# The opening's conditioning products: split tiles, another order of transfers

## The chip, the cores and the metric

The kernel runs on one NeuronCore of a Trainium2 chip. Its engines are TensorE (PE, matrix products), VectorE (DVE), ScalarE (ACT), GpSimd (POOL) and SyncE (SP, which issues most transfers). The metric is the device time of one execution in microseconds (us), lower is better, as a median of several runs.

## The reference

One step of a decoder layer over 2048 prompt positions and 8 sample rows, model width 1024. All is float32:

```
shift1,scale1,g1,shift2,scale2,g2 = silu(c) @ w_ada + b_ada      # c: 1 + 8 rows, w_ada: 1024 x 6144
h  = RMSNorm(x)*(1+scale1)+shift1
[u | q | k | v | a_pool | a_attn] = h @ w_in
x += g1 * ( sig(a_pool)*(PoolMix(u) @ w_pool_br) + sig(a_attn)*(DilatedAttn(q,k,v) @ w_attn_br) ) @ w_out
h2 = RMSNorm(x)*(1+scale2)+shift2
x += g2 * relu(h2 @ w_up)^2 @ w_down
```

The first line is the conditioning. Its 6144 columns make twelve blocks of 512. Blocks 0 and 1 are shift1, blocks 2 and 3 are scale1: block 0 and block 2 serve the channels of h's rows 0 to 3 (a row is 128 channels), blocks 1 and 3 those of rows 4 to 7. Only these four are needed before h exists; the other eight follow much later.

## The kernel before

Large products are done as three single-rate (float32r) products of split operands, high by high, high by low and low by high (`mm3`, lines 157 to 168); a weight tile is split by an ACT cast and a subtraction (`load_w`, lines 178 to 185). PE's order is written out by hand: it is the order of the `PE` calls in the code. The other engines' queues are ordered by the compiler from the code and its own planning, and each queue runs in order. SP issues the transfers. Weights come through `weights`, which loads one tile ahead from a fixed plan.

The work is done channel-major in two halves of the positions (`ci`); each half has two column groups, in the first half of 512 and 520 columns (`HALVES`; the 520 include the 8 samples). `opening` (line 723) runs ahead of the first half's q, k, v products. It does, for block b of 0, 2, 1, 3:

- `ada_load`: four transfers of 512 KB (a chunk: 128 x 1024, two row groups of the contraction) into raw tiles, of which there are eight;
- `ada_rows`: eight full float32 products of 9 rows (silu of c) by 512 columns, straight from the raw tiles, into one PSUM bank, and a copy to `arow`, a single buffer;
- `mod_block`, later in PE's order: four small products that turn the 9 x 512 row into columns; DVE adds the bias, and for blocks 2 and 3 forms the scales `scg`.

Between them stand the sum of squares of x (`x_sum`: ACT squares, DVE additions), its finish (`rms_finish`: a product with ones, square root, reciprocal), `make_h` (x times rs on DVE, scale and shift on ACT, a cast on ACT, a subtraction on DVE for even and POOL for odd rows), and `part(t)`: the first four of eight contraction steps of the four first q and k tiles, twelve products each, for 512 columns. The function returns the four open PSUM tiles; `qkv` then adds the other four steps (48 products), evicts each tile by two ACT instructions (L381, L382), and goes on with the 520 columns.

PE's order in the opening: block 0, sum of rs0, transposes of 0, block 2, its transposes, block 1, part 0, transposes of 1, part 1, block 3, sum of rs1, part 2, transposes of 3, part 3. The order of loads in the code: block 0, first columns of x, block 2, block 1, w_in, second columns of x, block 3.

A float32 product counts as two MATMUL records in the trace, so a block has 16 `ps_ada` records here.

Of the kernel before, what the change touches and what calls it, by code (L numbers as in the profile page):

```python
# [8 lines left out]
F32 = mybir.dt.float32  # L9
F32R = mybir.dt.float32r  # L10
AF = mybir.ActivationFunctionType
ALU = mybir.AluOpType
# [4 lines left out]
P = 128  # L17
D = 1024
KD = 8
# [10 lines left out]
HS_AT = 6500  # L30
ADA_GAP = 3600
DEPTH_O = 1
R1 = 2

BRS = (
# [79 lines left out]
def emit(tc, I, O):  # L115
    nc = tc.nc
    V, S, G, PE, SP = nc.vector, nc.scalar, nc.gpsimd, nc.tensor, nc.sync
# [3 lines left out]
    def pool(stack, name, bufs=1, space=None, side=None):  # L121
        kw = {}
        if space is not None:
            kw["space"] = space
        elif side is not None:
            kw["side"] = side
        if space is not DRAM:
            kw["reuse_waits"] = "tile"
        return stack.enter_context(tc.tile_pool(name=name, bufs=bufs, **kw))
# [5 lines left out]
    stp = pool(top, "stp", 2, PSUM)  # L135
# [13 lines left out]
    def first():  # L149
        return tc.high_priority(offset=PRIO)  # L150

    def mm(ps, w, x, start, stop, ns):
        PE.matmul(ps, w, x, start=start, stop=stop)  # L153
        od.spent(ns)
# [13 lines left out]
    def small(ps, w, x, ns=220.0):  # L168
        mm(ps, w, x, True, True, ns)
# [8 lines left out]
    def load_w(src, eng=G, rp=None, hq=None, n=1024, tag="wh"):  # L178
        raw = (rp or rawp).tile([P, 1024], F32, tag="wr", name="wr")
        SP.dma_start(out=raw[:, :n], in_=src)  # L180
        wt = (hq or hlp).tile([P, 2, n], F32R, tag=tag, bufs=1 if n < 1024 else None, name="wh")
        with first():
            S.copy(out=wt[:, 0, :n], in_=raw[:, :n])  # L183
            eng.tensor_tensor(out=wt[:, 1, :n], in0=raw[:, :n], in1=wt[:, 0, :n].bitcast(F32), op=ALU.subtract)  # L184
        return wt
# [27 lines left out]
    def weights(*key):  # L213

        i = issued[0] - len(ready)
        assert plan[i] == key, (plan[i], key)
        while issued[0] < len(plan) and issued[0] <= i + depth[0]:
            k = plan[issued[0]]
            src = I[k[0]][k[1]] if len(k) == 2 else I[k[0]][k[1], :, k[2] * 1024:(k[2] + 1) * 1024]
            ready.append(load_w(src, G, *(extra if issued[0] == 3 else ())))  # L220
            issued[0] += 1
        return ready.pop(0)
# [4 lines left out]
    cv = {}  # L227
    off = 0
    for name, shape in CPACK:
        n = int(np.prod(shape))  # L230
# [7 lines left out]
    cT, ident, ones, hones, mask = cv["cT"], cv["ident"], cv["ones"], cv["hones"], cv["mask"]  # L238
# [5 lines left out]
    sil = cst.tile([P, KD, 9], F32, name="sil")  # L244
    silr = cst.tile([P, KD, 2, 9], F32R, name="silr")
# [10 lines left out]
    def mod_block(b, row, nr, idn, psp, tag):  # L256

        pt = psp.tile([P, 512], F32, tag=tag, name="ps_mt")
        for j in range(4):
            small(pt[:, j * 9:(j + 1) * 9], row[0:nr, j * P:(j + 1) * P], idn)  # L260
        V.tensor_tensor(out=mod[:, 4 * b:4 * b + 4, :], in0=pt[:, 0:36].rearrange("p (j r) -> p j r", j=4),
                        in1=bada[:, 4 * b:4 * b + 4].to_broadcast([P, 4, 9]), op=ALU.add)
        for i, lo in ((0, 8), (1, 32)):
            j = 4 * b - lo
            if j in (0, 4):
                V.scalar_tensor_tensor(out=sc[:, i, j:j + 4, :], in0=mod[:, 4 * b:4 * b + 4, :], scalar=1.0,
                                       in1=gn[:, i, j:j + 4].to_broadcast([P, 4, 9]), op0=ALU.add, op1=ALU.mult)
# [23 lines left out]
    def rms_sum(np_, acc, x, n, first, eng):  # L291
        sq = np_.tile([P, 520], F32, tag="sq", bufs=3, name="sq")
        if first:
            S.activation(out=acc[:, :n], in_=x, func=AF.Square)
        else:
            S.activation(out=sq[:, :n], in_=x, func=AF.Square)
            eng.tensor_tensor(out=acc[:, :n], in0=acc[:, :n], in1=sq[:, :n], op=ALU.add)

    def rms_finish(np_, psp, acc, splits):
        rs = np_.tile([P, 520], F32, tag="rs", bufs=1, name="rs")  # L300
        for c0, n in splits:
            ps = psp.tile([P, 512], F32, tag="st", name="ps_st")
            small(ps[:, :n], ones, acc[:, c0:c0 + n], n / 0.6)
            S.activation(out=rs[:, c0:c0 + n], in_=ps[:, :n], func=AF.Sqrt, scale=1.0 / D, bias=epsc)
            V.reciprocal(out=rs[:, c0:c0 + n], in_=rs[:, c0:c0 + n])
        return rs
# [16 lines left out]
    mmp = pool(ps1, "mmp", 6, PSUM)  # L323
# [5 lines left out]
    def hx(hb, nk, c0, n):  # L329
        return [(hb[:, k, 0, c0:c0 + n], hb[:, k, 1, c0:c0 + n]) for k in range(nk)]  # L330
# [9 lines left out]
    def x_sum(ci, hi, xs, eng):  # L340
        n = HALVES[ci][hi][1]
        acc = npl.tile([P, 520], F32, tag="ssum", bufs=1, name="ssum")
        for k in range(KD):
            rms_sum(npl, acc, xs[k], n, k == 0, eng)
        return acc

    def make_h(ci, hi, xs, rs, hb, ks=range(KD)):
        c0, n, splits = HALVES[ci][hi]
        for k in ks:
            hf = npl.tile([P, 520], F32, tag="sq", bufs=3, name="hf")  # L350
            modulated(hf, xs[k], xs[k], rs, n, 0, k, hb, c0, ci == 0 and hi == 1, G if k % 2 else V)
# [8 lines left out]
    def new_h():  # L360
        return hp.tile([P, KD, 2, 1032], F32R, tag="h", name="h")
# [332 lines left out]
    h0 = new_h()  # L694

    def load_x0(op, hi):
        c0, n, _ = HALVES[0][hi]
        xt = op.tile([P, KD, 520], F32, tag="x0", bufs=2, name="x0")
        for k in range(0, KD, 2):
            SP.dma_start(out=xt[:, k:k + 2, :n], in_=I["xT"][k:k + 2, :, c0:c0 + n].rearrange("k p n -> p k n"))  # L700
        return [xt[:, k, :n] for k in range(KD)]

    def ada_load(op, b):
        out = []
        for kk in range(4):
            raw = op.tile([P, 1024], F32, tag="wr", bufs=8, name="wr")
            SP.dma_start(out=raw, in_=I["w_ada"][b, kk])
            out += [raw[:, 0:512], raw[:, 512:1024]]
        return out

    def ada_rows(op, b, raws):
        ps = mmp.tile([P, 512], F32, tag="mm", name="ps_ada")
        for k in range(KD):
            mm(ps[0:9, :], sil[:, k, :], raws[k], k == 0, k == KD - 1, 860.0)
        row = op.tile([9, 512], F32, tag="arow", bufs=1, name="arow")
        with first():
            S.copy(out=row, in_=ps[0:9, :])
        return lambda: mod_block(b, row, 9, ident[0:9, 0:9], stp, "st")

    def opening():  # L720

        ost = ExitStack()
        op = pool(ost, "open", side="left")
        raws = {0: ada_load(op, 0)}
        x0 = load_x0(op, 0)
        raws[2] = ada_load(op, 2)
        raws[1] = ada_load(op, 1)
        keys = [("w_in", 8 + 6 * qk + i) for qk in range(2) for i in range(2)]
        ws, pss = [weights(*keys[0])], []
        x1 = load_x0(op, 1)  # L730
        raws[3] = ada_load(op, 3)
        hxs = hx(h0, KD, 0, 512)

        def part(t):
            if t:
                ws.append(weights(*keys[t]))
            pss.append(mmp.tile([P, 512], F32, tag="mm", name="ps_qk"))
            mm3(pss[t], wk(ws[t], KD)[:4], hxs[:4], False, stop=False)

        m0 = ada_rows(op, 0, raws[0])  # L740
        acc = x_sum(0, 0, x0, V)
        rs0 = rms_finish(npl, stp, acc, HALVES[0][0][2])
        m0()
        m2 = ada_rows(op, 2, raws[2])
        m2()
        make_h(0, 0, x0, rs0, h0, range(4))
        m1 = ada_rows(op, 1, raws[1])
        acc = x_sum(0, 1, x1, V)
        part(0)
        m1()  # L750
        part(1)
        m3 = ada_rows(op, 3, raws[3])
        rs1 = rms_finish(op, stp, acc, HALVES[0][1][2])
        part(2)
        m3()
        make_h(0, 0, x0, rs0, h0, range(4, KD))
        make_h(0, 1, x1, rs1, h0)
        part(3)
        ost.close()
        return ws, pss  # L760

# [15 lines left out]
    for _ in range(2):  # L777
        b, kk = todo.pop(0)
# [51 lines left out]
    mmp = pool(psa, "mma", 2, PSUM)  # L830
# [371 lines left out]
    mmp = pool(ps3, "mm3", 6, PSUM)  # L1202
# [46 lines left out]
    def up(ci, f, hi, wt, hb):  # L1249
        c0, n, splits = HALVES[ci][hi]  # L1250
        rt = fp.tile([P, 2, 520], F32R, tag="rt", bufs=6, name="rt")
        for a, l in splits:
            ps = mmp.tile([P, 512], F32, tag="mm", name="ps_up")
            dense(ps, wt, hb, a, l)
            r1 = fp.tile([P, 512], F32, tag="r1", bufs=R1, name="r1")
            with first():
# [32 lines left out]
    for ci in range(2):  # L1289
# [15 lines left out]
        br = od.spawn(branches(ci, 1, hbs[1], GAP_B), 3000)  # L1305
        depth[0] = DEPTH_O
        acc = project(ci, 0, hbs[0], xa, load_xa)
# [11 lines left out]
        for fb in range(1, 16):  # L1319
            if fb == 1:  # L1320
                rts = [r0[2:], [r1[2], up(ci, 3, 1, weights("w_up", 3), hbs[1])]]
            else:
                rts = [[], []]
                for f in (2 * fb, 2 * fb + 1):
                    wt = weights("w_up", f)
# [123 lines left out]
```

## Time and profile before

| | us |
|---|---|
| median of 3 runs | 3072.97 (3070.19 to 3075.37) |
| profiled execution | 3068.15 |
| its span | 3066.3 |
| PE busy in the span | 2956.4 (96%) |
| DVE, ACT, POOL busy | 1590.4, 970.6, 960.6 |
| mean granted TensorE clock | 0.982 |

The span goes from the first to the last instruction. In the page's 40 slices of 77 us PE is at 7 tenths in the first, which holds the opening, and at 9 in most others; transfers move 239 GB/s in the first slice.

### The profile page before, as it was taken

The page shows a single profiled execution, that of the slowest core. Times are in us where ns is not written, and L with a number is a line of the kernel's source. Part 1 is how long each engine was busy: PE and PEld are TensorE (multiplying, and loading weights), DVE is VectorE, ACT ScalarE, POOL GpSimd, SP SyncE. Part 2 cuts the span into 40 slices and gives each one's busy share as a digit, 9 for nine tenths or more (in the row PEclk, how much of TensorE's full clock was granted, in tenths as well). Part 3 has the DMA queues.
Part 4 walks back from the last instruction along what each step waited for, and adds up shares of the span by engine and source line. Part 5 has one row for each costly group of instructions (what it writes and reads, how often), then busy time and mean ns, then how long its engine had stood idle before and what let it go on. Part 6 is the DMA issues. An engine that isn't in the chain of part 4 may idle for free.

```text
span 3066.3 us, 40880 instructions
## 1 busy us (share of the span) xinstructions
PE 2956.4 (96%) x16220; PEld 2526.4 (82%) x16220; DVE 1590.4 (52%) x2645; ACT 970.6 (32%) x1765; POOL 960.6 (31%) x504
## 2 busy tenths in 40 slices
PE   7999999999898799999999999999999999999999
PEld 3899788887787688887899999999877788888887
DVE  5656442542744524447865555545578554444444
ACT  4333332434544434433521221221235212111211
POOL 2565341433433311224531222122245312221221
PEclk9999999999899889999999999999999999999999
DMA  6544752335777878876221111111272211111111
GB/s 239 176 139 156 275 174 91 129 107 151 198 191 209 186 191 217 235 233 236 94 96 35 56 49 46 45 49 49 84 250 83 76 42 56 48 49 42 55 43 68
DMA packets 204431, 379.09 MB, mean 124 GB/s; under 512 B 43232, under 2 KB 99904, under 8 KB 203456
## 3 DMA queue, kind: packets, MB, share of 16 engines
q1 hardware_dynamic: 192720, 359.63, 38.2%
q10 hardware_dynamic: 11520, 16.85, 1.5%
q8 instruction: 128, 2.10, 0.3%
q14 instruction: 63, 0.52, 0.1%
HBM read 294.89 MB, written 81.75 MB: 123 GB/s over the span
## 4 chain that ended last, share of the span: by engine, by line
PE 77%; DMA 6%; DVE 5%; issue 3%; ACT 2%; POOL 2%; SPq 1%; DVEq 0%; ACTq 0%; POOLq 0%
PE ps_dn L153 22%; PE ps_up L153 22%; PE ps_g L153 9%; PE ps_qk L153 5%; PE ps_v L153 4%; PE ps_wo L153 4%; PE ps_u L153 3%; PE ps_s L153 2%; PE ps_o L153 1%; PE ps_pb L153 1%; POOL wh L184 1%; PE ps_ada L153 1%; PE ps_ab L153 1%; DMA t1d<-ta 1%; DMA cs<-in_rope 1%
## 5 line engine op out<-in xcount | busy, mean ns | idle before, releaser
L184 POOL TENSOR_TENSOR wh<-wr,wh 128x1024 fp32r<-128x1024 f32 (+1 forms) x274 | 650.1, 2380 | 1679.0 <-ACT wh L183 1607.5
L153 PE MATMUL ps_dn<-rt,wh 128*128 128x512 f32 (+2 forms) x3840 | 726.2, 350 | 6.4 <-POOL wh L184 3.3
L153 PEld LDWEIGHTS ps_dn<-rt,wh 128*128 128x128 f32 x3840 | 618.9, 188 | 109.2 <-POOL wh L184 4.2
L183 ACT CAST wh<-wr 128x1024 fp32r<-128x1024 f32 (+1 forms) x306 | 309.4, 1023 | 730.7 <-issue 562.3
L1274 DVE SCALAR_TENSOR_TENSOR xa<-ps_dn,mod,xa 128x512 f32<-128x512 f32 (+1 forms) x640 | 405.2, 641 | 202.8 <-PE ps_dn L153 201.0
L153 PE MATMUL ps_g<-h,wh 128*128 128x512 f32 (+2 forms) x1920 | 390.5, 355 | 0.4 <-POOL wh L184 0.4
L153 PE MATMUL ps_up<-hb,wh 128*128 128x264 f32 (+2 forms) x2304 | 371.5, 320 | 0.0
L153 PE MATMUL ps_up<-ha,wh 128*128 128x512 f32 x1536 | 365.7, 394 | 0.0
L153 PEld LDWEIGHTS ps_up<-hb,wh 128*128 128x128 f32 x2304 | 332.3, 188 | 36.0
L153 PEld LDWEIGHTS ps_g<-h,wh 128*128 128x128 f32 x1920 | 309.4, 191 | 48.4 <-POOL wh L184 0.9
L153 PEld LDWEIGHTS ps_up<-ha,wh 128*128 128x128 f32 x1536 | 287.1, 188 | 64.2 <-issue 0.5
L153 PE MATMUL ps_qk<-h,wh 128*128 128x512 f32 (+2 forms) x1440 | 301.1, 363 | 8.9 <-POOL h L318 6.5
L1258 DVE TENSOR_TENSOR r<-r 128x512 f32<-128x512 f32 (+2 forms) x160 | 99.3, 620 | 387.0 <-ACT r L1257 386.9
L153 PEld LDWEIGHTS ps_qk<-h,wh 128*128 128x128 f32 x1440 | 235.9, 194 | 50.8 <-POOL h L318 7.5
L1260 DVE TENSOR_TENSOR rt<-r,rt 128x512 fp32r<-128x512 f32 (+2 forms) x160 | 217.8, 1361 | 81.8 <-ACT rt L1259 81.7
L1257 ACT ACTIVATE r<-ps_up 128x512 f32<-128x512 f32 (+2 forms) x160 | 82.1, 513 | 415.0 <-PE ps_up L153 415.0
L153 PE MATMUL ps_v<-wh,h 128*128 128x256 f32 (+1 forms) x1224 | 169.3, 294 | 24.5 <-ACT wh L183 18.9
L153 PEld LDWEIGHTS ps_v<-wh,h 128*128 128x128 f32 (+1 forms) x1224 | 155.2, 192 | 30.2 <-ACT wh L183 19.3
L914 ACT ACTIVATE pe<-pe,ost 128x128 f32<-128x128 f32 (+1 forms) x192 | 87.1, 455 | 153.2 <-DVE ost L912 149.9
L912 DVE CUSTOM_DVE_ANT_0 pe<-ps_s,cp 128x128 f32<-128x128 f32 (+1 forms) x192 | 61.4, 358 | 129.7 <-PE ps_s L153 129.7
L1259 ACT CAST rt<-r 128x512 fp32r<-128x512 f32 (+2 forms) x160 | 85.8, 536 | 66.3 <-DVE r L1258 66.3
L153 PE MATMUL ps_pb<-py,wh 128*128 128x512 f32 (+2 forms) x480 | 95.5, 358 | 6.6 <-ACT py L555 3.7
(181 smaller groups left out, 2985.4 us busy)
## 6 DMA issues: line engine op xcount, KB each, us to landing
wr<-in_w_up SPq DMA_DIRECT2D x72, 512.0 KB
wr<-in_w_down SPq DMA_DIRECT2D x68, 512.0 KB
wr<-in_w_in SPq DMA_DIRECT2D x64, 512.0 KB
wr<-in_w_ada SPq DMA_DIRECT2D x48, 512.0 KB
slab<-kst SPq DMA_DIRECT2D x40, 512.0 KB
wr<-in_w_out SPq DMA_DIRECT2D x32, 512.0 KB
cs<-in_rope SPq DMA_DIRECT2D x18, 512.0 KB
qst<-ohl SPq DMA_DIRECT2D x9, 1024.0 KB
```

The source lines that it names most:

```text
L153: PE.matmul(ps, w, x, start=start, stop=stop)
L183: S.copy(out=wt[:, 0, :n], in_=raw[:, :n])
L184: eng.tensor_tensor(out=wt[:, 1, :n], in0=raw[:, :n], in1=wt[:, 0, :n].bitcast(F32), op=ALU.subtract)
L912: V.tensor_tensor_reduce(out=pe[:, off:off + nk], in0=ps[:, off:off + nk], in1=mask[:, mo:mo + nk], scale=-0.125, scalar=3.0e38, op0=ALU.a ...
L914: S.activation(out=pe[:, off:off + nk], in_=pe[:, off:off + nk], func=AF.Exp, scale=-1.0, bias=o[:, 64:65], accum_out=o[:, 65:66])
L1257: S.activation(out=r1[:, :l], in_=ps[:, :l], func=AF.Relu)
L1258: V.tensor_tensor(out=r1[:, :l], in0=r1[:, :l], in1=r1[:, :l], op=ALU.mult)
L1259: S.copy(out=rt[:, 0, a:a + l], in_=r1[:, :l])
L1260: V.tensor_tensor(out=rt[:, 1, a:a + l], in0=r1[:, :l], in1=rt[:, 0, a:a + l].bitcast(F32), op=ALU.subtract)
L1274: V.scalar_tensor_tensor(out=x[:, c0 + a:c0 + a + lp], in0=ps[:, :lp], scalar=mod[:, 40 + m, 0:1], in1=x[:, c0 + a:c0 + a + lp], op0=ALU.m ...
```

## The change

All four blocks of the opening are now done from split tiles: of each chunk ACT makes a cast (high part), and DVE, or POOL for every third chunk (number 1, 4, 7, 10, 13 of 16), the rest (low part). Each of a chunk's two contraction steps is then two single-rate products of 18 rows (`silr`: high and low part of silu of c), so a block has 16 products, and the transposes also add the two sets of 9 rows (`fold`). There are four raw tiles instead of eight and two split tiles; the load of chunk t+4 is issued behind the split of chunk t (`fetch`).

The order changes too. Transfers in the code: block 0, first columns of x, blocks 2, 1 and 3 as their raw tiles come free, the first two w_in, second columns of x, the other w_in. PE's order: block 0, block 2, sum of rs0, transposes of 0 and 2, block 1, its transposes, part 0, block 3, its transposes, parts 1, 2, 3, sum of rs1. `x_sum` of the second columns stands behind part 2.

```diff
--- before.py
+++ after.py
@@ -30,6 +30,7 @@
 HS_AT = 6500
 ADA_GAP = 3600
 DEPTH_O = 1
+OPEN_RAW = 4
 R1 = 2
 
 BRS = (
@@ -700,62 +701,75 @@
             SP.dma_start(out=xt[:, k:k + 2, :n], in_=I["xT"][k:k + 2, :, c0:c0 + n].rearrange("k p n -> p k n"))
         return [xt[:, k, :n] for k in range(KD)]
 
-    def ada_load(op, b):
-        out = []
-        for kk in range(4):
-            raw = op.tile([P, 1024], F32, tag="wr", bufs=8, name="wr")
-            SP.dma_start(out=raw, in_=I["w_ada"][b, kk])
-            out += [raw[:, 0:512], raw[:, 512:1024]]
-        return out
-
-    def ada_rows(op, b, raws):
-        ps = mmp.tile([P, 512], F32, tag="mm", name="ps_ada")
-        for k in range(KD):
-            mm(ps[0:9, :], sil[:, k, :], raws[k], k == 0, k == KD - 1, 860.0)
-        row = op.tile([9, 512], F32, tag="arow", bufs=1, name="arow")
-        with first():
-            S.copy(out=row, in_=ps[0:9, :])
-        return lambda: mod_block(b, row, 9, ident[0:9, 0:9], stp, "st")
-
     def opening():
 
         ost = ExitStack()
         op = pool(ost, "open", side="left")
-        raws = {0: ada_load(op, 0)}
-        x0 = load_x0(op, 0)
-        raws[2] = ada_load(op, 2)
-        raws[1] = ada_load(op, 1)
+        order = [(b, kk) for b in (0, 2, 1, 3) for kk in range(4)]
+        raws, taken = [], [0]
+
+        def fetch(n):
+            for b, kk in order[len(raws):len(raws) + n]:
+                raw = op.tile([P, 1024], F32, tag="wr", bufs=OPEN_RAW, name="wr")
+                SP.dma_start(out=raw, in_=I["w_ada"][b, kk])
+                raws.append(raw)
+
+        def ada_rows(b):
+
+            ps = mmp.tile([P, 512], F32, tag="mm", name="ps_ada")
+            for kk in range(4):
+                t = taken[0]
+                assert order[t] == (b, kk)
+                raw, wt = raws[t], op.tile([P, 2, 1024], F32R, tag="wh", bufs=2, name="wh")
+                S.copy(out=wt[:, 0], in_=raw)
+                (G if t % 3 == 1 else V).tensor_tensor(out=wt[:, 1], in0=raw, in1=wt[:, 0].bitcast(F32), op=ALU.subtract)
+                fetch(1)
+                taken[0] += 1
+                for j in range(2):
+                    k = 2 * kk + j
+                    lhs = silr[:, k].rearrange("p l r -> p (l r)")
+                    for hl in range(2):
+                        mm(ps[0:18, :], lhs, wt[:, hl, j * 512:(j + 1) * 512], k == 0 and hl == 0, k == KD - 1 and hl == 1, 216.0)
+            row = op.tile([18, 512], F32, tag="arow", bufs=1, name="arow")
+            with first():
+                S.copy(out=row, in_=ps[0:18, :])
+            return lambda: mod_block(b, row, 18, cv["fold"][0:18, :], stp, "st")
+
         keys = [("w_in", 8 + 6 * qk + i) for qk in range(2) for i in range(2)]
-        ws, pss = [weights(*keys[0])], []
-        x1 = load_x0(op, 1)
-        raws[3] = ada_load(op, 3)
+        ws, pss = [], []
         hxs = hx(h0, KD, 0, 512)
 
         def part(t):
-            if t:
-                ws.append(weights(*keys[t]))
             pss.append(mmp.tile([P, 512], F32, tag="mm", name="ps_qk"))
             mm3(pss[t], wk(ws[t], KD)[:4], hxs[:4], False, stop=False)
 
-        m0 = ada_rows(op, 0, raws[0])
+        fetch(OPEN_RAW)
+        x0 = load_x0(op, 0)
+        m0 = ada_rows(0)
         acc = x_sum(0, 0, x0, V)
+        m2 = ada_rows(2)
         rs0 = rms_finish(npl, stp, acc, HALVES[0][0][2])
         m0()
-        m2 = ada_rows(op, 2, raws[2])
         m2()
-        make_h(0, 0, x0, rs0, h0, range(4))
-        m1 = ada_rows(op, 1, raws[1])
+        make_h(0, 0, x0, rs0, h0, range(2))
+        m1 = ada_rows(1)
+        make_h(0, 0, x0, rs0, h0, range(2, 4))
+        ws.append(weights(*keys[0]))
+        m1()
+        part(0)
+        m3 = ada_rows(3)
+        x1 = load_x0(op, 1)
+        ws.append(weights(*keys[1]))
+        m3()
+        part(1)
+        make_h(0, 0, x0, rs0, h0, range(4, KD))
+        ws.append(weights(*keys[2]))
+        part(2)
         acc = x_sum(0, 1, x1, V)
-        part(0)
-        m1()
-        part(1)
-        m3 = ada_rows(op, 3, raws[3])
+        ws.append(weights(*keys[3]))
+        part(3)
         rs1 = rms_finish(op, stp, acc, HALVES[0][1][2])
-        part(2)
-        m3()
-        make_h(0, 0, x0, rs0, h0, range(4, KD))
         make_h(0, 1, x1, rs1, h0)
-        part(3)
         ost.close()
         return ws, pss
```

## Rows read from the trace of the kernel before

**Rows 1.** The page's chain that ended last, by engine.
```profile
PE 77%; DMA 6%; DVE 5%; issue 3%; ACT 2%; POOL 2%; SPq 1%; DVEq 0%; ACTq 0%; POOLq 0%
```

**Rows 2.** Timeline of PE, 0 to 140 us: start, duration, instruction, count, idle before.
```profile
6.40 8.53 PE L153 MATMUL ps_ada<-wr,sil 128*9 128x512 f32 x16 [6.40 <-DVE silr L254]
18.82 1.24 PE L153 MATMUL ps_st<-ssum,cp 128*128 128x512 f32 x2 [3.89 <-DVE ssum L297]
...
21.80 9.37 PE L153 MATMUL ps_ada<-wr,sil 128*9 128x512 f32 x16
...
32.87 7.03 PE L153 MATMUL ps_ada<-wr,sil 128*9 128x512 f32 x16
...
44.68 0.73 PE L153 MATMUL ps_qk<-h,wh 128*128 128x512 f32 x2 [0.19 <-POOL h L318]
...
46.33 3.05 PE L153 MATMUL ps_qk<-h,wh 128*128 128x512 f32 x12
...
56.27 1.15 PE L153 MATMUL ps_st<-ssum,cp 128*128 128x256 f32 x4
...
60.12 1.05 PE L153 MATMUL ps_mt<-cp,arow 9*128 9x9 f32 x8
...
88.87 6.70 PE L153 MATMUL ps_qk<-h,wh 128*128 128x256 f32 x32 [3.69 <-POOL h L318]
```

**Rows 3.** Timeline of ACT, 0 to 100 us.
```profile
5.05 0.26 ACT L246 ACTIVATE sil<-cp 128x72 f32<-128x72 f32 x1 [3.04 <-DMA cp<-in_cpack]
...
15.83 1.66 ACT L296 ACTIVATE sq<-x 128x512 f32<-128x512 f32 x3
...
33.97 1.52 ACT L312 ACTIVATE hf<-x,mod,scg 128x512 f32<-128x512 f32 x2 [2.14 <-DVE scg L266]
...
62.21 1.53 ACT L312 ACTIVATE hf<-x,mod,scg 128x512 f32<-128x512 f32 x2 [3.41 <-DVE scg L266]
...
83.57 0.68 ACT L317 CAST h<-hf 128x520 fp32r<-128x520 f32 x1
```

**Rows 4.** Windows: stretch, busy by engine (instructions), PE clock, DMA share, GB/s.
```profile
0.00:10.00 10.00, 3.60 (x5) 0.63 (x6) 0.99 (x6) 1.80 (x3) 0.20 (x4) 1.00 0.80 291
10.00:20.00 10.00, 6.11 (x15) 1.22 (x13) 4.84 (x7) 6.24 (x10) 0.00 (x0) 0.98 1.02 399
```

**Rows 5.** Timeline of all engines, 291 to 300 us, where later blocks are split.
```profile
290.95 5.76 POOL L184 TENSOR_TENSOR wh<-wr,wh 128x1024 fp32r<-128x1024 f32 x2 [4.22 <-ACT wh L183]
...
293.23 4.57 DVE L184 TENSOR_TENSOR wh<-wr,wh 128x1024 fp32r<-128x1024 f32 x2 [1.62 <-ACT wh L183]
...
298.69 1.08 PE L153 MATMUL ps_ada<-wh,silr 128*18 128x512 f32 x4
```

**Rows 6.** Groups of ACT, 0 to 90 us: count, busy us, mean ns, idle before.
```profile
L312 ACT ACTIVATE hf<-x,mod,scg 128x520 f32<-128x520 f32 x8 | 6.1, 813 | 1.5 <-POOL h L318 1.5
...
L317 ACT CAST h<-hf 128x520 fp32r<-128x520 f32 x8 | 4.8, 631 | 0.8 <-DVE hf L315 0.8
...
L183 ACT CAST wh<-wr 128x1024 fp32r<-128x1024 f32 x4 | 4.1, 1037 | 0.0
```

**Rows 7.** Line 184, whole span: count, ns least/median/most, first and last start.
```profile
L184 POOL TENSOR_TENSOR wh<-wr,wh x274: 1272/2400/3396, 37.0 to 3030.5; 128x1024 fp32r<-128x1024 f32 x134, 128x512 fp32r<-128x512 f32 x3
L184 DVE TENSOR_TENSOR wh<-wr,wh x32: 1205/1225/3423, 293.2 to 485.4; 128x1024 fp32r<-128x1024 f32 x32
```

**Rows 8.** Timeline of SP's queue: first issue, time until the last is issued.
```profile
0.74 0.39 SPq L226 DMA_DIRECT2D cp<-in_cpack  x1
...
6.28 10.16 SPq L707 DMA_DIRECT2D wr<-in_w_ada  x8
17.28 1.56 SPq L180 DMA_DIRECT2D wr<-in_w_in  x2
```

**Rows 9.** Groups of DVE, 0 to 90 us.
```profile
L297 DVE TENSOR_TENSOR ssum<-ssum,sq 128x520 f32<-128x520 f32 x7 | 8.1, 1162 | 0.5
...
L305 DVE RECIPROCAL rs<-rs 128x512 f32<-128x512 f32 x1 | 3.3, 3343 | 0.0
```

## The prediction

> **What bounds the kernel now.** First the chain of waits: 77% of the span is TensorE (PE) [rows 1], so a microsecond that the opening gives or takes reaches the end as long as the later stages wait for PE. I then read the opening, some 90 us, engine by engine, because all that the change edits lies there. PE's own timeline [rows 2] is the frame. Block 0's sixteen half-product records run from 6.40 to 14.93, block 2's from 21.80 to 31.17, block 1's to 39.90; the first w_in product (part 0) waits for h until its last two products end at 45.41; block 3's transposes end at 61.17; and PE starts again only at 88.87, when the last h of the second 520 columns is there. From then on it runs through. So the question is when that last h exists after the change. The timeline of ScalarE (ACT) says why it is late now: its last cast runs at 83.57 [rows 3]. Transfers are the early limit: 291 GB/s in the first 10 us and 399 in the next, with a DMA share of 1.02 [rows 4].
>
> **Part by part.** All times are from the profiled span, 3066.3; its execution took 3068.15, so 1.85 lie around it, and the median of the three runs, 3072.97, is 4.8 above that execution. I add the difference found here to either.
>
> *The products.* Sixteen records of a block take 7.03 at full clock and 9.37 after a pause [rows 2]. The same kind of block later in this kernel, split and single-rate, takes 1.08 for the four products of a chunk [rows 5], about 0.9 without the last one's tail: 3.6 a block, a saving of 3.4. At half clock I take 1.7 a chunk; the pause of 3.9 ahead of block 2 (14.93 to 18.82) cost 9.37 - 7.03 = 2.3 now.
>
> *The split that each chunk needs.* One ACT cast, 1.04 [rows 6]; one subtraction, 1.22 on VectorE (DVE) or 2.4 on GpSimd (POOL), both medians [rows 7]. Chunks 1, 4, 7, 10 and 13 go to POOL. There are two split tiles, so chunk t's cast waits for PE's products of chunk t-2. A link of that chain is 1.04 + 1.22 + 0.9 = 3.2, or 4.4 by POOL, and 0.8 more at half clock. Two links a block, in two interleaved strands, make 7 to 8 us: the product time saved on PE comes back as waiting.
>
> A DVE subtraction beside one of POOL is not 1.22: two and two together, begun at 290.95, ended at 297.80, DVE's at 2.28 each and POOL's at 2.88 [rows 5]. I take 1.9 for the one in block 2 that meets POOL's. The Trainium skill ("SBUF — State Buffer", section "SBUF: two separate sides") says that the ports these two engines share are an exclusive lock, and the loser waits for the whole instruction. Four in turn would be 7.2, near the 6.85 seen; by that rule block 2 would end 0.7 later than below.
>
> *Block 0.* The constants' transfer, issued at 0.74, is read at 5.05 [rows 8, 3]. Cast 0 stands behind the conditioning vector's own cast, which PE had used by 6.40: I take 6.15 to 7.2, DVE to 8.45, products to 10.15. Chunk 1 comes from POOL at 10.6, products to 12.3. Cast 2 waits for 10.15, cast 3 for 12.3; the block ends at about 16 (14.93 before).
>
> *Block 2.* Its transfers go out when chunks 0 to 3 have been split (8.5 to 14.6), behind x. At 10 us 2.9 MB are there, then 0.4 MB/us [rows 4]: constants, block 0 and x are 4.9 MB, so x ends near 15 and the four chunks land at 16.3 to 20.2, one per 1.3. ACT has the squares of x until 17.5 [rows 3], one cast later with one between: cast 4 at 18.5, POOL to 21.9, products to 23.6 at half clock; chunk 5 to 25.3; cast 6 waits for 23.6, products to 26.8; cast 7 waits for 25.3, POOL to 28.8; the block ends at 29.7 (31.17).
>
> *rs0, moved behind block 2.* In PE's fixed order the sum of squares (1.24), block 0's transposes (1.05), a copy on ACT (0.55, a third of 1.66 [rows 3]) and block 2's transposes (1.05) follow: 33.7. The reciprocal, 3.34 [rows 9], formerly under block 2's products, begins at 31.7 and ends at 35.1; one x*rs, and the first modulated row is at 36.3 (33.97 before [rows 3]): 2.3 lost.
>
> *Block 1.* Chunks 8 and 9 have been split by then; 10 goes through POOL to 38.0, and the block ends at 39.7 (39.90).
>
> *The transfers' order.* SP issues these loads in the order of the code: eight w_ada, of which four wait for PE, take it 10.16, and the w_in behind them, free from the start, went out only after them [rows 8]. So w_in now stands behind chunk 15, whose slot is free when chunk 11 has been split: issue at 39.1. A transfer that is not queued took 5.05 - 0.74 for 0.69 MB (the code's shapes) [rows 8, 3]; less 1.7 for its bytes that leaves 2.6, or 3.9 for half a megabyte. Chunks 14 and 15 and the first w_in land at 41.9, 43.2 and 44.5; cast and POOL to 47.9; part 0 to 51.0. Before, it ended at 45.41. The second columns of x follow and land near 50, under block 3.
>
> *Block 3.* Two chunks are ready; 14 and 15 wait for the products of 12 and 13: 5.3, to 56.3. After copy, transposes and sums the scales for h 4 to 7 exist at 58.6; before, h 4 began at 62.21 [rows 3]. This is the gain, 3.6.
>
> *The tail.* Parts 1 to 3, 3.05 each [rows 2], go from 58.0 to 67.2 over h 4 to 7, and rs1's sum, 1.15, follows in PE's order, at 68.4; before, it was out of the way at 57.4 [rows 2]. Then 0.5, a reciprocal of 3.4, one multiplication: second columns from 73.1. ACT gives each of eight rows 0.81 + 0.63 [rows 6], 11.5 together, and between them the evictions of three of the four tiles, a pair like these two each, 4.2: 88.8, a subtraction of 1.2 to 1.7, and PE goes on at 90.0 against 88.87. That is +1.1: the head start of 3.6 is spent because rs1 begins behind part 3 instead of ahead of block 3's transposes.
>
> At no cost: copy and transposes of 18 rows instead of 9 (same columns; 0 to 0.1 a block, under no cover); the number and bytes of transfers, unchanged. The rope tiles reuse the opening's memory and may now wait for the second columns of x: 0 (the rope work of the first half can be late by the 12 us of products behind it) to 2 (one more row of POOL's in the way); I take 0. The shift past 90 us I take as carried whole; -2 to +2 for stretches where PE waits for others.
>
> **Rivals.** *Faster: transfers and splits are hidden.* If w_in and x go ahead of waiting w_ada in SP's order, or chunk 15's slot comes early, part 0 ends near 45.4 with h: 5.6 earlier, so -4.5. If also casts come at landing and PE stays at full clock, block 2 ends at 24.6, the first h is at 31.2, and the sum is near -8. For it: no single product or transfer left is long. Against it: [rows 8], the two split tiles, and a clock that fell after one pause of 3.9. Time: 3065 to 3068.5.
>
> *Slower: the second columns' squares come late.* The code puts their sum behind part 2, and ACT runs its queue in order. If they stand there behind h 4 to 7, they begin at 66.5; with seven additions at 1.16 [rows 9] the sum is there at 75, at the squares' own pace (1.66 for three) at 72. PE, in whose order rs1's sum stands ahead of the 48 remaining products, waits for it from 67.2, and the tail starts 5 to 8 later: +6 to +9, 3079 to 3082. It decides from the point where the first square runs later than about 60. For it: the order of the code. Against it: x lands near 50, and ACT is idle while block 3 waits for its slots.
>
> *No effect* is the forecast itself: two moves that cancel.
>
> **How the numbers follow.** The forecast has 0.53: 3072.97 + 1.1 = 3074.1, its own range 3070 to 3078. Hiding has 0.26, late squares 0.21. What can be told from no change here is 0.2%, 6.1 us. The faster case is beyond that in its upper half, the slower one nearly whole, and the opening's schedule is known to some 2 us a block, which adds to both tails: faster 0.25, same 0.53, slower 0.22. The range is 3063.5 (-8, less 1.5 for the runs' spread) to 3083 (+9 and 1).
>
> **What would show it.** Right: ps_ada products in groups of four with pauses of 1 to 2 us; block 2 ended at 28 to 31; the first w_in issued after the sixteenth w_ada, near 39; part 0 not before 45; h 4 near 59; rs1 behind part 3; PE through near 90. Wrong: part 0 ended before 44, or the pause ahead of the second columns over before 84 (faster); PE waiting for the sum of squares behind part 3 (slower).

## The result, and the profile after

The change made the kernel slower. After takes 3091.55 us (median of 4 runs, 3086.71 to 3095.70) and before, on the same chip, 3071.58 (4 runs, 3068.09 to 3075.37): a ratio of 1.0071 with the interval 1.0058 to 1.0084, or 20 us. The forecast was 3074.1 in 3063.5 to 3083; the time lies above the range. The profiled execution of after is 3095.7, of which the span is 3093.6.

The page of after: its span, busy times, PE's first slices and clock, and the chain that answers to [rows 1].

```profile
span 3093.6 us, 40936 instructions
...
PE 2957.8 (96%) x16220; PEld 2531.0 (82%) x16220; DVE 1612.3 (52%) x2656; ACT 987.3 (32%) x1781; POOL 972.6 (31%) x509
...
PE   6799999999899889999999999999999999999999
...
PEclk7899999999999989999999999999999999999999
...
PE 76%; DVE 6%; DMA 4%; issue 4%; ACT 3%; POOL 2%; SPq 1%; ACTq 0%; DVEq 0%; POOLq 0%
```

PE is busy as long as before (2957.8 against 2956.4), so what is lost is waiting. To find where, I use one point in time, called the mark: the start of the first long run of 32 products over the second columns, from which PE runs on with one wait that is not short (for the rope squares: 1.70 before, 3.77 after). It is the last row of [rows 2], 88.87 before. After, it is 110.50, a shift of 21.6, so nearly all of the loss arises ahead of it. What lies behind it is not carried exactly: the first gate product, a later point, comes at 315.19 instead of 290.99 (24.2), and the profiled execution of after, the slowest of its four, is 27.6 above that of before, where the medians are 20.0 apart. The timeline of PE after (start, duration, records, idle before and its releaser) shows the way there:

```profile
15.44 0.87 PE L154 MATMUL ps_ada<-wh,silr 128*18 128x512 f32 x3 [0.30 <-DVE wh L725]
...
29.25 1.47 PE L154 MATMUL ps_ada<-wh,silr 128*18 128x512 f32 x3 [1.79 <-POOL wh L725]
...
39.97 3.05 PE L154 MATMUL ps_ada<-wh,silr 128*18 128x512 f32 x7 [1.49 <-POOL wh L725]
...
45.97 0.65 PE L154 MATMUL ps_qk<-h,wh 128*128 128x512 f32 x1 [0.88 <-ACT h L318]
47.69 1.65 PE L154 MATMUL ps_qk<-h,wh 128*128 128x512 f32 x3 [1.06 <-DVE h L319]
51.59 1.65 PE L154 MATMUL ps_qk<-h,wh 128*128 128x512 f32 x3 [2.26 <-POOL h L319]
57.18 2.50 PE L154 MATMUL ps_qk<-h,wh 128*128 128x512 f32 x5 [3.94 <-DVE h L319]
...
67.06 1.06 PE L154 MATMUL ps_mt<-cp,arow 18*128 18x9 f32 x8 [0.66 <-ACT arow L735]
68.05 8.61 PE L154 MATMUL ps_qk<-h,wh 128*128 128x512 f32 x36
82.43 2.07 PE L154 MATMUL ps_st<-ssum,cp 128*128 128x256 f32 x4 [5.78 <-DVE ssum L298]
...
104.68 2.08 PE L154 MATMUL ps_hs<-qsq,cp 128*128 128x512 f32 x2 [5.14 <-POOL qsq L397]
...
110.50 5.62 PE L154 MATMUL ps_qk<-h,wh 128*128 128x256 f32 x32 [2.48 <-POOL h L319]
```

Blocks 0, 2 and 1 end at 16.3, 30.7 and 43.0; part 0, in four pieces that each wait for a row of h, at 59.7; the sum for rs1 makes PE wait 5.78 behind part 3. For the piece at 57.18, the queues of DVE and POOL:

```profile
46.95 0.68 DVE L319 TENSOR_TENSOR h<-hf,h 128x512 fp32r<-128x512 f32 x1
47.55 8.97 DVE L312 TENSOR_TENSOR x<-x,rs 128x512 f32<-128x512 f32 x4
56.45 0.68 DVE L319 TENSOR_TENSOR h<-hf,h 128x512 fp32r<-128x512 f32 x1
...
68.38 2.10 DVE L267 SCALAR_TENSOR_TENSOR scg<-mod,cp 128x36 f32<-128x36 f32 x1
...
76.11 6.18 DVE L298 TENSOR_TENSOR ssum<-ssum,sq 128x520 f32<-128x520 f32 x7 [0.37 <-ACT sq L297]
```

```profile
46.95 2.91 POOL L185 TENSOR_TENSOR wh<-wr,wh 128x1024 fp32r<-128x1024 f32 x1 [1.00 <-ACT wh L184]
49.82 3.41 POOL L319 TENSOR_TENSOR h<-hf,h 128x512 fp32r<-128x512 f32 x2
53.19 2.79 POOL L725 TENSOR_TENSOR wh<-wr,wh 128x1024 fp32r<-128x1024 f32 x1
...
107.04 1.72 POOL L397 TENSOR_TENSOR qsq<-qsq 128x512 f32<-128x512 f32 x1
108.72 1.72 POOL L319 TENSOR_TENSOR h<-hf,h 128x520 fp32r<-128x520 f32 x1
```

In DVE's queue the x*rs of rows 4 to 7, which nothing needs before 68, stand ahead of the subtraction for row 2, which PE needs next. Alone they take 0.69 each (they do before, over 16). Here they take 2.24, because POOL works without a break from 46.95 to 55.98 on four instructions, 9.1 in all: four of DVE's for four of POOL's. The small scale at 68.38 takes 2.10 beside POOL's split at 68.04; it takes 0.20 elsewhere. Two-input operations of the two engines here go in turn, instruction by instruction. The Trainium skill ("SBUF — State Buffer", section "SBUF: two separate sides"), which the prediction named, says that whichever of the two starts first holds the shared ports for its whole instruction, and the other waits. The trace agrees with it.

The timeline of ACT after, with the idle time before each row:

```profile
43.90 1.51 ACT L313 ACTIVATE hf<-x,mod,scg 128x512 f32<-128x512 f32 x2
...
50.69 0.63 ACT L295 ACTIVATE ssum<-x 128x520 f32<-128x520 f32 x1
61.43 1.04 ACT L724 CAST wh<-wr 128x1024 fp32r<-128x1024 f32 x1 [10.11 <-PE ps_ada L154]
...
70.52 1.52 ACT L313 ACTIVATE hf<-x,mod,scg 128x512 f32<-128x512 f32 x2 [2.56 <-DVE scg L267]
...
75.44 1.16 ACT L297 ACTIVATE sq<-x 128x520 f32<-128x520 f32 x2
...
88.42 2.25 ACT L313 ACTIVATE hf<-x,mod,scg 128x520 f32<-128x520 f32 x3 [3.39 <-DVE x L312]
...
105.19 0.68 ACT L318 CAST h<-hf 128x520 fp32r<-128x520 f32 x1
```

The first modulated row is 9.9 later than before (33.97, [rows 3]). At 51.3 ACT comes to the cast of chunk 14, whose split tile PE frees only in block 3, and the whole queue stands for 10.11: of the eight squares one ran ahead of it, and the seven behind it begin at 75.44, after h 4 to 7. The last row of h is cast at 105.19 to 105.87, but POOL subtracts it only from 108.72 to 110.44, behind rope instructions, and the mark follows. Finally, windows of 20 us of the opening of after (busy by engine, PE clock, DMA share, GB/s):

```profile
20.00:40.00 20.00, 13.80 (x44) 5.22 (x45) 12.77 (x10) 9.74 (x10) 7.05 (x3) 0.67 0.55 190
40.00:60.00 20.00, 10.84 (x29) 5.56 (x30) 15.40 (x13) 9.80 (x14) 11.39 (x5) 0.59 0.78 291
```

PE had pauses in both stretches, and the granted clock was 0.67 and 0.59, so mostly the lower of its two levels (1.2 GHz). Part 0's twelve products take 6.45 (0.65 + 1.65 + 1.65 + 2.50); at full clock they took 3.05 [rows 2].

### The profile page after: what moved, and what is told of

Read it like the earlier page. It is cut to its first block, busy times and chain, and to the rows that moved or that the text cites. A ratio compares the mean times of both kernels' runs of the same rounds, so it can differ in the third digit from the quotient of the medians.

```text
span 3093.6 us, 40936 instructions
## 1 busy us (share of the span) xinstructions
PE 2957.8 (96%) x16220; PEld 2531.0 (82%) x16220; DVE 1612.3 (52%) x2656; ACT 987.3 (32%) x1781; POOL 972.6 (31%) x509
## 4 chain that ended last, share of the span: by engine, by line
PE 76%; DVE 6%; DMA 4%; issue 4%; ACT 3%; POOL 2%; SPq 1%; ACTq 0%; DVEq 0%; POOLq 0%
PE ps_dn L154 22%; PE ps_up L154 22%; PE ps_g L154 10%; PE ps_qk L154 5%; PE ps_v L154 4%; PE ps_u L154 3%; PE ps_wo L154 3%; PE ps_o L154 2%; PE ps_s L154 1%; PE ps_pb L154 1%; POOL wh L185 1%; DMA slab<-kst 1%; PE ps_ada L154 1%; PE ps_t L173 1%; ACT wh L184 1%
## 5 line engine op out<-in xcount | busy, mean ns | idle before, releaser
L154 PEld LDWEIGHTS ps_v<-wh,h 128*128 128x128 f32 (+1 forms) x1224 | 156.7, 194 | 29.7 <-ACT wh L184 19.4
```

## The experiments

All times are us. "Mark" is as above and "gate" is the first gate product, both read from one profile. The kernel before, run along with these, had a median of 3073.51 beside e1 to e4, 3071.88 beside e5 to e8 and 3071.48 beside e9 and e10. Where a ratio is given, the kernel ran 4 to 10 times; the others have one run.

| kernel | mark | gate | time | ratio to before |
|---|---|---|---|---|
| before | 88.87 | 290.99 | | |
| after | 110.50 | 315.19 | 3091.55 | 1.0071 (1.0058 to 1.0084) |
| e1 split products, order of before | 102.41 | 304.32 | 3086.58 | 1.0036 (1.0020 to 1.0051) |
| e2 whole products, order of after | 93.71 | 298.52 | 3079.00 | 1.0014 (1.0001 to 1.0028) |
| e3 after, rs0 in its former place | 108.33 | 313.05 | 3091.89 | |
| e4 after, rs1 early | 103.78 | 304.59 | 3089.57 | |
| e5 after, chunks' subtractions all on DVE | 103.18 | 307.93 | 3086.93 | |
| e6 after, three split tiles | 102.72 | 307.64 | 3090.14 | |
| e7 after, none of these subtractions on POOL | 96.02 | 296.33 | 3075.11 | |
| e8 e2 with rs1 early | 85.53 | 286.67 | 3065.70 | 0.9973 (0.9963 to 0.9983) |
| e9 e7 with rs1 early | 90.45 | 295.97 | 3075.73 | 1.0013 (1.0003 to 1.0022) |
| e10 e8, none of these subtractions on POOL | 76.75 | 282.18 | 3064.13 | 0.9975 (0.9963 to 0.9986) |

**The change in two halves: e1 and e2.** e1 keeps the split products and takes back the order; e2 keeps the order, with whole float32 products from eight raw tiles.

```diff
# e1 against after
         acc = x_sum(0, 0, x0, V)
-        m2 = ada_rows(2)
         rs0 = rms_finish(npl, stp, acc, HALVES[0][0][2])
         m0()
+        m2 = ada_rows(2)
...
-        make_h(0, 0, x0, rs0, h0, range(2))
+        ws.append(weights(*keys[0]))
+        x1 = load_x0(op, 1)
+        make_h(0, 0, x0, rs0, h0, range(4))
         m1 = ada_rows(1)
+        acc = x_sum(0, 1, x1, V)
+        part(0)
+        m1()
...
# e2 against after
-                S.copy(out=wt[:, 0], in_=raw)
-                (G if t % 3 == 1 else V).tensor_tensor(out=wt[:, 1], in0=raw, in1=wt[:, 0].bitcast(F32), op=ALU.subtract)
...
-                    for hl in range(2):
-                        mm(ps[0:18, :], lhs, wt[:, hl, j * 512:(j + 1) * 512], k == 0 and hl == 0, k == KD - 1 and hl == 1, 216.0)
+                    mm(ps[0:9, :], sil[:, k, :], raw[:, j * 512:(j + 1) * 512], k == 0, k == KD - 1, 860.0)
```

> Split tiles and single-rate products as in the changed kernel, but every call of the opening in the order of the kernel before (rs0 and its transposes ahead of block 2, w_in and the second columns of x ahead of block 3's transfers, their sum and rs1 ahead of part 2). The mark is when PE goes through into the second columns after its last wait for h: 88.9 before, 110.5 after. Theory A, the order of the queues costs: it is near 90 (87 to 95), the run within 6 us of before. Theory B, the splits cost (a cast, a subtraction and two split tiles in the way of each chunk): it is near 105, the run 15 us or more slower than before.

> Whole float32 products from eight raw tiles as before, but the calls in the order of the changed kernel (the second four transfers behind x). Theory A (order): the same mark near 105 (100 to 110), PE waiting 4 us or more for rs1's sum of squares behind part 3, the run 12 us or more slower than before. Theory B (splits): near 90, within 6 us of before.

The order alone moves the mark by +4.8, the splits alone by +13.5, both by +21.6; 3.3 more than the sum. In the medians the order costs 5.5 and the splits 13.1. The splits cost most. In e1, DVE's queue again:

```profile
29.88 1.16 DVE L725 TENSOR_TENSOR wh<-wr,wh 128x1024 fp32r<-128x1024 f32 x1
30.95 8.98 DVE L312 TENSOR_TENSOR x<-x,rs 128x512 f32<-128x512 f32 x4
39.86 1.21 DVE L725 TENSOR_TENSOR wh<-wr,wh 128x1024 fp32r<-128x1024 f32 x1
```

Block 1 runs from 35.84 to 53.4 there, because a chunk's subtraction stands behind 8.98 of x*rs slowed by POOL. In e2 the loss of the order is one row of PE, the wait for rs1's sum behind part 3:

```profile
53.17 8.60 PE L154 MATMUL ps_qk<-h,wh 128*128 128x512 f32 x36
65.72 2.07 PE L154 MATMUL ps_st<-ssum,cp 128*128 128x256 f32 x4 [3.94 <-DVE ssum L298]
```

**Single places in the order: e3 and e4.**

```diff
# e3 against after
-        m2 = ada_rows(2)
         rs0 = rms_finish(npl, stp, acc, HALVES[0][0][2])
         m0()
+        m2 = ada_rows(2)
         m2()
# e4 against after
         x1 = load_x0(op, 1)
+        acc = x_sum(0, 1, x1, V)
+        rs1 = rms_finish(op, stp, acc, HALVES[0][1][2])
         ws.append(weights(*keys[1]))
         m3()
...
-        acc = x_sum(0, 1, x1, V)
         ws.append(weights(*keys[3]))
         part(3)
-        rs1 = rms_finish(op, stp, acc, HALVES[0][1][2])
```

> The changed kernel with one edit: rs0 and block 0's transposes again ahead of block 2. If rs0 behind block 2 costs: the reciprocal begins near 22 instead of 36, the first modulated row is near 36 instead of 43.9, part 0 ends near 53 instead of 59.7 and the mark falls from 110.5 to about 104. If the casts waiting in ACT's queue cost instead: the first modulated row stays at 41 or later and the mark at 108 or later.

> The changed kernel with one edit: the sum of squares of the second columns stands in the code behind their load and rs1's product ahead of block 3's transposes. If the late squares cost: PE's wait of 5.8 us behind part 3 is gone, the reciprocal runs before 78 instead of 84 to 88, and the mark falls from 110.5 to 101 to 104. If the tail is bound by ACT's rows anyway: the wait goes, but the mark stays at 107 or later.

rs0's place is worth 2.2 of the mark (the time, one run, is 18.4 above before): a small part of the cause. The reciprocal is back at 26.82, but the first modulated row comes at 43.78, only 0.1 earlier than in after. DVE's x*rs take 8.97 beside POOL, and on ACT a chunk's cast that waits for PE stands ahead of the row:

```profile
31.16 8.97 DVE L312 TENSOR_TENSOR x<-x,rs 128x512 f32<-128x512 f32 x4
```

```profile
42.83 1.05 ACT L724 CAST wh<-wr 128x1024 fp32r<-128x1024 f32 x1 [4.91 <-PE ps_ada L154]
43.78 1.52 ACT L313 ACTIVATE hf<-x,mod,scg 128x512 f32<-128x512 f32 x2
```

An early rs1 is worth 6.7, but only in part: with the splits in the way, PE now waits for the same sum ahead of block 3's transposes.

```profile
70.89 2.10 PE L154 MATMUL ps_st<-ssum,cp 128*128 128x256 f32 x4 [7.07 <-DVE ssum L298]
```

**The shared turns: e5 and e7.** The work stays, its engine changes.

```diff
# e5 against after
-                (G if t % 3 == 1 else V).tensor_tensor(out=wt[:, 1], ...
+                V.tensor_tensor(out=wt[:, 1], ...
# e7: e5, and
-            ready.append(load_w(src, G, *(extra if issued[0] == 3 else ())))
+            ready.append(load_w(src, V if issued[0] < 4 else G, *(extra if issued[0] == 3 else ())))
...
-            modulated(..., G if k % 2 else V)
+            modulated(..., G if k % 2 and ci else V)
```

> The changed kernel, with the five chunk subtractions of GpSimd given to VectorE as well. The mark (PE through into the second columns) was 110.5. Theory C, VectorE and GpSimd take turns on two-input work, so a GpSimd subtraction of 2.4 costs VectorE 2.4: eleven to sixteen subtractions of 1.2 on VectorE alone are shorter in all, and the mark falls to 104 to 108. Rival D, VectorE's queue is the limit by its length: it gets five more instructions, and the mark stays at 110 or later.

> The changed kernel with no work at all on GpSimd in the opening: chunk subtractions, those of the first four w_in tiles and those of h are on VectorE. Theory C (taking turns): x times rs takes 0.69 for each of the sixteen instead of 2.24 for the four beside GpSimd's work, part 0 ends near 52 to 55 instead of 59.7, the mark falls to 100 to 105. Rival D (length of VectorE's queue): part 0 ends at 59 or later and the mark stays at 110 or later.

Both marks went the way the theory of shared turns said, and beyond its ranges (104 to 108 for e5, 100 to 105 for e7). In e7 DVE gets five chunks, four w_in splits and eight rows of h more to do, and PE is through 14.5 earlier (part 0 ends at 49.9 instead of 59.7). In e7, DVE's subtractions for rows 2 and 3, its x*rs and the small scale:

```profile
46.68 1.29 DVE L319 TENSOR_TENSOR h<-hf,h 128x512 fp32r<-128x512 f32 x2
47.89 2.49 DVE L312 TENSOR_TENSOR x<-x,rs 128x512 f32<-128x512 f32 x4
...
59.16 0.20 DVE L267 SCALAR_TENSOR_TENSOR scg<-mod,cp 128x36 f32<-128x36 f32 x1
```

The four x*rs take 2.49 in all instead of 8.97, and the scale 0.20 again. That PE is through sooner although DVE took over the other's work rules out the length of DVE's queue as the limit. How much of the two gains is turns is not told apart from two other things. POOL is slower by itself: alone, a chunk's subtraction takes it 2.35, and DVE 1.23. In e5 the reciprocal begins 5.6 earlier than in after, before POOL has split anything:

```profile
30.52 3.35 DVE L306 RECIPROCAL rs<-rs 128x512 f32<-128x512 f32 x1
```

And in e7 the order of DVE's queue is another: the subtractions for rows 2 and 3 stand ahead of the x*rs of rows 4 to 7. No run took away the meetings alone.

**The casts that wait for PE: e6.** Three split tiles, and three raw ones for the room; rs1's tiles come from another pool of memory.

```diff
-OPEN_RAW = 4
+OPEN_RAW = 3
-                raw, wt = raws[t], op.tile([P, 2, 1024], F32R, tag="wh", bufs=2, name="wh")
+                raw, wt = raws[t], op.tile([P, 2, 1024], F32R, tag="wh", bufs=3, name="wh")
-        rs1 = rms_finish(op, stp, acc, HALVES[0][1][2])
+        rs1 = rms_finish(npl, stp, acc, HALVES[0][1][2])
```

> The changed kernel with three split tiles and three raw tiles instead of two and four (four of each do not fit the memory; rs1 is kept in rs0's buffer to make room). Theory E, ACT's queue standing still behind casts that wait for PE's products two chunks back costs most: ACT's waits on ps_ada products, 23.9 us in all before the mark, fall below 12, the first modulated row is at 38 or earlier, the mark at 100 to 105. Rival C (turns of VectorE and GpSimd): the waits fall, the mark stays within 2 of 110.5.

The mark is in the middle of what was expected for the casts; the first modulated row is at 39.90, later than the 38 named. ACT's waits for a slot, which were 23.9 in 11 in after, are gone, and waits for transfers stand in their place (the first column of sums is total, times, longest):

```profile
ACT wh L724 <- DMA wr<-in_w_ada: 10.0, 9, 4.8
```

So the slots are a second cause in the opening; three of them are worth 7.8 of the mark, with one raw tile less. The time, one run, is 18.3 above its before where after was 20.0; after's own four runs lie within 9, so one run can't say whether the 7.8 reached the end (at the gate 7.6 of it are left).

**What is left without splits, and with both cures: e8, e9 and e10.** e8 is e2 with the edit of e4, e9 is e7 with the edit of e4, e10 is e8 with the last two lines of e7's edit.

> Whole float32 products in the new order as in the second run, and the sum of squares of the second columns and rs1's product moved ahead of block 3's transposes. There the scales for h 4 to 7 exist at about 54 instead of 62 before. If only the late sum spent that head start: the wait of 3.9 behind part 3 goes, the mark falls from 93.7 to 82 to 86 and the run is 3 to 7 us (0.1 to 0.2%) faster than before. If the tail is bound by ACT and GpSimd whatever comes first: the mark is at 89 or later and the run not faster than before.

> The split products in the new order with two edits together: no two-input work on POOL in the opening (alone: PE through at 96.0 instead of 110.5), and the second columns' sum of squares and rs1 ahead of block 3's transposes (alone: 103.8). Theory C (the splits' own casts and subtractions, with ACT's casts waiting for PE, remain as a floor): the sum wait left in the off-POOL kernel was only 1.8, so the two gains overlap; PE through at 92 to 96, time 3 to 7 us above the kernel before. Rival W (what is left is the late sum and nothing else): the gains add up, 14.5 + 6.7; PE through below 90.5, the time equal to before or faster.

> Whole fp32 products in the new order with rs1 early (alone: PE through at 85.5, ratio 0.9973), and the opening's w_in splits and h subtractions moved from POOL to DVE. Theory T (the two engines' taking turns is what cost the time, whatever they split): PE through 2 to 5 earlier, 80 to 83, ratio below 0.996. Theory Q (DVE's queue is the limit when the chunks' subtractions are in it, and without them POOL's share is help): PE through at 85 to 89, ratio 0.997 or above.

e8 beats before by 0.27%: the new order is a gain, once the one thing that it made late is put early. Its PE has no wait for the sum, and is through at 85.53:

```profile
53.00 1.15 PE L154 MATMUL ps_st<-ssum,cp 128*128 128x256 f32 x4
54.26 1.05 PE L154 MATMUL ps_mt<-cp,arow 9*128 9x9 f32 x8
```

e9 brings the split products near before's level, not to it or below: 0.13% slower, and the interval (1.0003 to 1.0022) leaves out 1. At the mark the two gains add up nearly (20.1 of 21.2), as the rival said, and the floor that the other theory named is not there, though PE still waits 4.20 for rs1's sum. At the gate they do not: 295.97 against e7's 296.33. There e9 is 5.0 behind before, because a later wait of PE for the rope squares is 5.07 where it is 1.70 before; the time, 4.2 above before, is in the range of the floor for this other reason. The split products gained nothing in any arrangement tried; e9 and e10, which differ in them and in the raw tiles, are 13.7 apart at the mark.

e10 is the surprise. The mark is 8.8 earlier than in e8, below even what the theory of turns expected, and the clock stays up (1.00 in the windows 20 to 40 and 40 to 60). Yet the ratio is that of e8, not below 0.996 as that theory had it. A wait behind the mark has taken part of it back; the third row is the first gate product, a point that before reaches at 290.99 and e8 at 286.67:

```profile
76.75 5.59 PE L154 MATMUL ps_qk<-h,wh 128*128 128x256 f32 x32 [2.75 <-DVE h L319]
...
112.20 1.13 PE L154 MATMUL ps_hs<-qsq,cp 128*128 128x264 f32 x2 [4.41 <-POOL qsq L397]
...
282.18 7.86 PE L154 MATMUL ps_g<-h,wh 128*128 128x512 f32 x42
```

The rope squares of the second columns come late (in e8 the same wait is 1.70). The trace shows most of the reason, and it is a turn once more. ACT's evictions that make these squares wait for DVE's rope work on the tile before, and its first product meets a w_in split of POOL. In e10, and last the same product in e8:

```profile
105.95 2.38 POOL L185 TENSOR_TENSOR wh<-wr,wh 128x1024 fp32r<-128x1024 f32 x1
106.03 2.59 DVE L402 TENSOR_TENSOR ro<-ab,cs 128x264 f32<-128x264 f32 x1 [4.88 <-POOL ohl L425]
```

```profile
114.25 0.43 DVE L402 TENSOR_TENSOR ro<-ab,cs 128x264 f32<-128x264 f32 x1 [4.37 <-POOL ohl L425]
```

That is 2.2 of the 2.7 by which the wait is longer; in e9 the same product takes 2.58 beside a split of 2.37. Of 8.8 over e8, 4.5 are left at the gate. In the medians, each against its own before, 1.2 are left (7.4 against 6.2), which the intervals don't tell from none. What takes the other 3 is open: no run was made for it.

## Why the prediction was wrong, point by point

It forecast the mark at 90.0, and it came at 110.50: 20.5 to explain. Against the prediction's own points, in order: part 0 ended 8.7 later (59.7, not 51.0); from there to the scales for h 4 to 7, 3.2 more (10.8, not 7.6); from the scales to the first modulated row of the second columns 3.4 more (17.9, not 14.5); from there to PE 5.2 more (22.1, not 16.9). The sum is 20.5.

- **The chain of chunks was right for two blocks.** Cast, subtraction, products, with two slots: 16, 29.7 and 39.7 were forecast for blocks 0, 2, 1, and 16.3, 30.7 and 43.0 came. The 1.0 at block 2 is near the 0.7 that the prediction gave for strict turns. Block 1 is 3.3 late: POOL was through with chunk 10 at 39.91, not 38.0, and chunk 11's subtraction stood behind the reciprocal in DVE's queue, to 40.99.
- **"One x*rs, and the first modulated row is at 36.3" failed, by 7.6.** The reciprocal began at 36.11, not 31.7. On ACT a copy of block 2's row waited for PE's transposes, and the square root with its table load (1.28) stood behind it. Then DVE had a chunk's subtraction ahead of x*rs (to 40.99), and ACT a chunk's cast, one of w_in and a copy ahead of the row (41.52 to 43.98). The term had the path of the data, and not the queues that it runs in. rs0's move itself is not the reason: with rs0 in its former place (e3) the row comes at 43.78, 0.1 earlier.
- **"Part 0 to 51.0" is the step that failed most: it came at 59.7.** Part of it is the late row (43.90); from that row to the end of part 0 it then took 15.8, where before took 11.4 (33.97 to 45.41). The transfer was no limit: one w_in went out at 35.24, ahead of two of the last w_ada, so the queue's order was not the code's either. Part 0 waited for h. The prediction costed the x*rs of rows 4 to 7 at nothing, did not ask where they stand in DVE's queue, and gave the price of meeting POOL to a single subtraction (1.9 for 1.22), though [rows 5] showed every instruction of such a meeting stretched. In e7 the meeting is gone, and so are those x*rs from ahead of row 2, and part 0 ends at 49.9; which of the two did more is not shown.
- **Block 3: 5.3 forecast, 6.9 measured.** The first nine products took 3.96, at a granted clock of 0.53 (59.5 to 63.5), the lower level; the forecast comes out with 0.9 a chunk, the pace of the higher one. Behind the block, a scale of 0.20 took 2.10.
- **"rs1's sum, at 68.4" failed, by the slower rival.** The rival said that the squares stand behind h 4 to 7 in ACT's queue, and that it decides from a first square later than 60. One square came at 50.69, the other seven from 75.44, and PE waited 5.78 for the sum, within the 5 to 8 given. It had 0.21; the argument against it, that ACT is idle while block 3 waits for slots, was wrong in kind: an in-order queue that waits for a slot is not idle, it is closed. e2 shows the same wait without any split (3.94), and e8 removes it.
- **The tail, 16.9 forecast, 22.1 measured: a term mis-sized by 3.4.** The evictions and rows share ACT as was said, and its last cast ended 17.4 after the first row (15.7 forecast). From that cast to PE the prediction gave one subtraction, 1.2; it took 4.6, because the row is POOL's and stands in its queue behind rope instructions. The change did not do this: before, the last cast ends at 84.25 [rows 3] and PE goes on at 88.87 [rows 2], 4.6 as well. The reading that ACT's last cast says why the mark is late stopped one instruction short. PE's wait of 5.14 for the rope squares lies inside this stretch and does not end it.
- **The range** took the rivals one at a time, with 2 us a block for the schedule. What happened was the slower rival on top of errors of 8.7 and 3.4 in the forecast itself. All three come from queues, and all have the same sign: what stands ahead in an in-order queue was costed at nothing.

The shift past 90 us was taken as carried whole. In after it nearly was (21.6 at the mark, 24.2 at the gate, 20.0 in the medians), but it is not safe: e9's shift grows from 1.6 to 5.0 at the gate, and e10 keeps 7.4 of 12.1.

## What to carry to other kernels

When work is added to ACT, DVE or POOL in a latency-bound stage, write out each queue in order, and ask of every instruction that waits which ones are shut in behind it; a cast for a buffer that is not free closes ACT to work that is ready. Cost two-input work on DVE and POOL in the same stretch as one queue, not two. When a stage is re-ordered, find the one result that has become late and move its inputs, too: here that turned +0.14% into -0.27%.

## What the runs showed of the hardware that was not expected

- How far the turns go: a 36-column operation of 0.20 took 2.10 and ended at 70.48, with POOL's split (68.04 and 2.40, to 70.44); in e5 it took 2.10 beside a split as well. The price is what POOL's instruction has left, not the size of DVE's.
- Moving two-input work from POOL to DVE made the opening shorter with split products and with whole ones (e5 and e7, e10), although DVE was the busier engine: 84.28 against 51.11 in the first 125 us of after.
- PE's clock is part of the price of pauses: 0.67 and 0.59 in two windows of after, 0.84 in 20 to 40 before, 1.00 in both in e10.
